# Weight sums of the down product: in place on VectorE instead of on GpSimd

## The chip, the cores and the metric

The kernel runs on one core of one Trainium2 chip. The metric is the device time of one execution in microseconds (us), the median of several runs. The engines are PE (matrix products), PEld (its weight loads), ACT (ScalarE), DVE (VectorE), POOL (GpSimd) and SP, whose queue issues the DMAs.

## What is computed

One block of a hybrid decoder in float32: 16 meta tokens and 1024 tokens of 1024 features, a state-space mixer and differential attention side by side, a merge, and then a gated feed-forward stage with a short convolution. The change lies in the last product of that stage, `@ w_down`:

```python
D_FF = ((8 * D_MODEL // 3 + 127) // 128) * 128      # 2816 = 22 blocks of 128

def conv_glu_ffn(h, w_up, conv_w, conv_b, w_down):
    seq_len = h.shape[1]
    up = h @ w_up
    a, b = up[..., :D_FF], up[..., D_FF:]
    a_pad = jnp.pad(a, ((0, 0), (CONV_W - 1, 0), (0, 0)))
    c = (a_pad[:, 0:seq_len] * conv_w[0] + a_pad[:, 1:seq_len + 1] * conv_w[1]
         + a_pad[:, 2:seq_len + 2] * conv_w[2] + conv_b)
    return (jax.nn.gelu(c) * b) @ w_down

h = h + conv_glu_ffn(rmsnorm(h, norm2_g[l]), w_up[l], conv_w[l], conv_b[l], w_down[l])
```

## The kernel before

Features lie on the partitions, tokens in the columns. Products in float32 accuracy are made of three matmuls: each operand is split in a high part (a copy on ACT, line 103) and a low part (a subtraction on VectorE, line 91), and high times high, high times low and low times high are added up in PSUM.

`ffn_up` (line 961) makes the up product with Strassen's scheme in Winograd's form: `Quad` objects, each with seven products. VectorE adds the products out of PSUM (`plus`, tiles `u2` to `u4` and `T`), GpSimd multiplies the gated halves (`times`, `crow<-crow,T`) and then forms three mixtures of the result (`mix`, tiles `T`), which SP stores to DRAM as `d_act`, `d_t2`, `d_t3`, `d_t4`.

`ffn_down` (line 1022) uses the same scheme for the down product. The weight `w_down` comes as 22 blocks `wd` of 128 x 1024, one DMA each; block f holds the left half of the columns (A11(f), 512 wide) and the right half (A21(f)); block f + 11 holds A12(f) and A22(f). The seven products run in this order, with these weights:

1. A11
2. S3 = A11 - A21
3. A12
4. A22
5. S2 = A21 + A22 - A11
6. S1 = A21 + A22, which the kernel before keeps in A21's place
7. S4 = A12 - S2, in A12's place

Each product is a loop over 11 steps f (`product`, line 1052). A step loads 128 x 512 of data (`act`, SP), splits it into `bop` (ACT, then VectorE), splits the weight into `wop` (`wop`, line 1014: ACT, then VectorE) and issues 12 matmuls of 512 columns into four PSUM tiles (line 181). In the program's order PE has the four high-times-high matmuls of a step first, then those with low parts (from f = 2 of the first product on). `bop` has two buffers (tag R of `rowp`) in the first product and five in the others (R and three of tag bo); `wop` has six. At a product's end ACT or VectorE adds the four PSUM tiles to the running sums (`quarter`, `h`).

Before the change the sums are made by GpSimd, at the place in the code where the product that uses them asks for its weight:

```python
def S3(f):
    s = self.wp.tile([128, 8, 128], F32, tag="raw", name="s3")[:, 0:4]
    self.tt(s, A11(f), A21(f), ALU.subtract, eng=G)
    return s
```

S3 goes into one of two buffers (tag raw), and S2 and S4 are formed in place. A scheduler sets the order of each engine's instructions from these data dependences: in it GpSimd's sums for S2 and S4 stand as soon as their operands are there, between those for S3.

Of the kernel before, what the change touches and what calls it, by code (L numbers as in the profile page):

```python
# [18 lines left out]
T = NM + SEQ  # L19
# [48 lines left out]
class Pool:  # L68
    """A tile pool whose tags have the numbers of buffers given."""
# [13 lines left out]
class Block:  # L83
# [24 lines left out]
    def splitter(self, i):  # L108
        """The engine that takes the low part of the i-th weight block after the attention's start."""
        return self.nc.gpsimd if i >= POOL_FROM else None  # L110

    def load_w(self, ap, eng=None):
        """A weight block of 128 partitions x 1024 columns, split in two parts of 12 bits each."""
# [9 lines left out]
    def mm3(self, ps, terms):  # L123
        """ps = sum of w^T b over (w_hi, w_lo, b_hi, b_lo), in float32 accuracy."""
        n = 3 * len(terms)
        i = 0
        for wh, wl, bh, bl in terms:
            for w, b in ((wh, bh), (wh, bl), (wl, bh)):
                self.nc.tensor.matmul(out=ps, lhsT=w, rhs=b, start=(i == 0), stop=(i == n - 1))  # L129
                i += 1  # L130
# [4 lines left out]
    def split(self, src, hi, lo, scale=None):  # L135
        """hi + lo = src * scale, each of 12 significant bits."""
# [7 lines left out]
    def rms_row(self, acc, n, e_row=None):  # L144
        """The row of 1 / rms on every partition, from the sum of squares over the feature tiles
        (a Newton step on the tables' value of v ** -0.5)."""
# [17 lines left out]
    def lin(self, jobs, tag="mm", late=0):  # L164
        """jobs: (columns, terms) each; one PSUM tile each, all of them open at once; the last `late` terms of
        every job come after the others."""
# [101 lines left out]
    def start(self):  # L268
        """Loads, the splits of h, the first two blocks of u (by k, as h comes in), and the row of 1 / rms."""
# [80 lines left out]
    def qk_block(self, h, qk):  # L350
        """Columns of q or k, normed over the 64 of each half; -2 times them, in fact (the gains make up for it)."""
# [44 lines left out]
    def fill_lin(self, jobs, tiles=None, late=0, outer=False):  # L396
        """As lin, as a generator that yields after the products of each k their time in us; ends with the tiles."""
# [16 lines left out]
    def gates(self):  # L414
        self.wnext = self.load_w(self.a["w_in"][16])
        for i in range(16):
# [16 lines left out]
            else:  # L433
                # by k, so that y takes the places of h as they come free
# [15 lines left out]
    def exp_small(self, x, n, pool, want_em1=None):  # L450
        """exp(x) for x [128, n] (clamped to [-87, 88]); with want_em1 [128, m]: exp(x) - 1 of the first m."""
# [23 lines left out]
    def small_params(self):  # L475
        """lam, and the gains with the constants that go with them."""
# [23 lines left out]
    def ssm(self):  # L500
# [37 lines left out]
        # unit phases and powers 1, 2, 4, 8  # L538
# [31 lines left out]
        # f = (lambda - 1) / a  # L570
# [19 lines left out]
        # signs: the upper half of the partitions holds real parts, the lower imaginary ones  # L590
# [7 lines left out]
        for b in range(4):  # L598
# [11 lines left out]
            # rotation tables e^{i phi (j + 1)}  # L610
# [18 lines left out]
            # Z[states, (m, c')] = lambda^m B  # L629
# [11 lines left out]
            # C lambda^(n+1)  # L641
# [9 lines left out]
            # the kernel's first 8 lags  # L651
# [22 lines left out]
            # chunk inflows, rotated into a frame in which the states only decay  # L674
# [39 lines left out]
    def load_y(self):  # L714
# [7 lines left out]
        # twice gelu, by tanh  # L722
# [58 lines left out]
    def attention(self, fill):  # L781
        """Per step: the scores of one block of queries, the weighted values of the one before, and other
        products between them, as many as hide the softmax."""
# [84 lines left out]
    def w_o(self):  # L868
        """h2 = h + mixed w_o, the first half of the tokens before the second; its rows end up normed."""
# [60 lines left out]
    def operand(self, pool, tag, src, eng=None):  # L930
        """src in two parts of 12 bits each."""
# [6 lines left out]
    def mixtures(self):  # L938
        """The operands of h for the seven products of Strassen's scheme in Winograd's form, the halves being
        those of the features and those of the tokens (which overlap by the two that the convolution needs)."""  # L940
# [73 lines left out]
    def wop(self, w):  # L1014
        """A weight operand of four tiles, in two parts of 12 bits each."""
# [6 lines left out]
    def ffn_down(self):  # L1022
        """The same scheme over halves of the hidden features, of the columns and of the tokens."""
# [14 lines left out]
        def S3(f):  # L1038
            s = self.wp.tile([128, 8, 128], F32, tag="raw", name="s3")[:, 0:4]
            self.tt(s, A11(f), A21(f), ALU.subtract, eng=G)  # L1040
            return s

        def S2(f):
            self.tt(A21(f), A21(f), A22(f), ALU.add, eng=G)
            self.tt(A11(f), A21(f), A11(f), ALU.subtract, eng=G)
            return A11(f)

        def S4(f):
            self.tt(A12(f), A12(f), A11(f), ALU.subtract, eng=G)
            return A12(f)  # L1050

        def product(w, src):
            tiles = [self.psum("mm", [128, n]) for _ in range(4)]
            for f in range(NQ):
# [13 lines left out]
                for m in range(4):  # L1068
                    self.mm3_term(tiles[m], (wh[:, m], wl[:, m], t[:, 0], t[:, 1]), f == 0, f == NQ - 1)
            return tiles  # L1070
# [14 lines left out]
        tiles = product(A11, act(0, 0))  # L1085
# [399 lines left out]
```

## Time and profile before

| | us |
|---|---|
| median of 3 runs | 1481.39 |
| lowest, highest | 1480.11, 1489.38 |
| span of the profiled execution, first to last instruction | 1480.3 |
| first matmul of the down product (line 181, 512 columns) | 1252.44 |
| end of its last matmul | 1474.6 |

The profiled execution's own time is given by its span alone; the median of the runs is 1.1 us above it. Times in the views are counted from the start of the span. A row of a timeline gives the start, the length, the engine, the line (L91 is the helper for VectorE's and GpSimd's two-operand instructions, L103 that for ACT, L129 and L181 are matmuls), what is written and what is read, and in brackets the idle time before it with what ended it. Where a row says x3, its length covers all three. Tile names there have no numbers: `s` is the sum S3, `wd` a weight block or a sum in its place.

### The profile page before, as it was taken

The numbers are of one execution on the slowest core, as the hardware profiler recorded it, in microseconds if no ns is written. First come the engines' busy times: TensorE is split into PE (matmuls) and PEld (weight loads), VectorE is DVE, ScalarE is ACT, GpSimd is POOL, SyncE is SP. The second block draws the span as 40 slices with busy tenths as digits, with TensorE's granted clock in tenths as the row PEclk, the third lists the DMA queues.
The fourth block names the chain that finished last, engine by engine and source line by source line (L and its number), as shares of the span: only waits on it lengthen the run. The fifth ranks groups of instructions, "written<-read, shape, count | busy, mean of one in ns | idle before, by whom it ended". The sixth has DMA issues, their size and how long they took to land.

```text
span 1480.3 us, 23053 instructions
## 1 busy us (share of the span) xinstructions
PE 1419.1 (96%) x8714; PEld 1305.3 (88%) x8714; DVE 1033.7 (70%) x1838; ACT 612.2 (41%) x1144; POOL 601.7 (41%) x517
## 2 busy tenths in 40 slices
PE   8979998999999899999999699999999999989998
PEld 7979898999999798999998698999999998767887
DVE  8948677535646778548366997767767676888574
ACT  6233443345545476433253443333333332433442
POOL 2176565321111301000224666555655557695030
PEclk9999999999999999999999799999999999999999
DMA  5423433472433424567432022233333336925341
GB/s 193 140 75 110 125 112 106 138 187 72 111 104 106 122 67 139 171 237 247 136 129 93 30 78 97 98 107 100 101 107 107 108 114 261 381 70 163 122 128 57
DMA packets 75615, 190.48 MB, mean 129 GB/s; under 512 B 9072, under 2 KB 20720, under 8 KB 75504
## 3 DMA queue, kind: packets, MB, share of 16 engines
q1 hardware_dynamic: 75504, 189.01, 39.7%
q8 instruction: 68, 1.11, 0.3%
q14 instruction: 43, 0.35, 0.1%
HBM read 130.13 MB, written 53.41 MB: 124 GB/s over the span
## 4 chain that ended last, share of the span: by engine, by line
PE 66%; DVE 12%; DMA 7%; POOL 6%; issue 4%; ACT 3%; SPq 2%; DVEq 0%; ACTq 0%; POOLq 0%
PE ps_mm L181 32%; PE ps_mm L129 26%; PE po L1355 3%; POOL rot L91 1%; POOL COS L91 1%; PE s L1319 1%; PE wt L1364 1%; POOL SIN L91 1%; PE s L1320 1%; DMA act<-d_t 1%; DVE wop L91 1%; POOL wd L91 1%; DVE B L91 1%; DMA zs<-z 1%; DMA qkvrow<-d_qkv 1%
## 5 line engine op out<-in xcount | busy, mean ns | idle before, releaser
L129 PE MATMUL ps_mm<-B,wop 128*128 128x256 f32 (+2 forms) x2772 | 443.8, 323 | 14.5 <-DVE B L91 6.8
L129 PEld LDWEIGHTS ps_mm<-B,wop 128*128 128x128 f32 x2772 | 401.4, 192 | 56.6 <-DVE B L91 8.1
L181 PE MATMUL ps_mm<-bop,wop 128*128 128x512 f32 x924 | 215.0, 393 | 9.2 <-DVE bop L91 5.5
L181 PEld LDWEIGHTS ps_mm<-bop,wop 128*128 128x128 f32 x924 | 172.8, 187 | 51.2 <-DVE bop L91 6.3
L181 PE MATMUL ps_mm<-hhi,whi 128*128 128x342 f32 (+2 forms) x432 | 138.3, 331 | 1.8 <-ACT hhi L103 1.8
L181 PE MATMUL ps_mm<-hlo,whi 128*128 128x342 f32 (+2 forms) x432 | 139.6, 323 | 0.1
L181 PE MATMUL ps_mm<-hhi,wlo 128*128 128x342 f32 (+2 forms) x432 | 139.1, 323 | 0.0
L91 POOL TENSOR_TENSOR wlo<-wraw,whi 128x1024 fp32r<-128x1024 f32 x18 | 44.7, 2481 | 205.6 <-ACT whi L103 190.2
L91 POOL TENSOR_TENSOR crow<-crow,T 128x512 f32<-128x512 f32 x44 | 69.8, 1599 | 112.8 <-DVE T L91 112.8
L129 PE MATMUL ps_mm<-hhi,whi 128*128 128x348 f32 (+3 forms) x336 | 113.0, 336 | 0.0
L129 PE MATMUL ps_mm<-hlo,whi 128*128 128x348 f32 (+3 forms) x336 | 110.5, 329 | 0.0
L129 PE MATMUL ps_mm<-hhi,wlo 128*128 128x348 f32 (+3 forms) x336 | 110.1, 328 | 0.0
L91 DVE TENSOR_TENSOR wop<-S,wop 128x512 fp32r<-128x512 f32 x66 | 64.9, 984 | 63.0 <-ACT wop L103 63.0
L91 DVE TENSOR_TENSOR bop<-act,bop 128x512 fp32r<-128x512 f32 x77 | 77.0, 1006 | 39.4 <-ACT bop L103 39.4
L103 ACT ACTIVATE whi<-wraw 128x1024 fp32r<-128x1024 f32 (+3 forms) x62 | 62.1, 1003 | 98.4 <-PE ps_mm L181 49.5
L91 DVE TENSOR_TENSOR wop<-wraw,wop 128x512 fp32r<-128x512 f32 x88 | 86.9, 991 | 13.7 <-ACT wop L103 13.2
L103 ACT ACTIVATE wop<-S 128x512 fp32r<-128x512 f32 x66 | 40.0, 626 | 133.4 <-POOL S L91 96.5
L1321 DVE CUSTOM_DVE_ANT_0 S<-s,bias 128x348 f32<-128x348 f32 (+9 forms) x120 | 57.7, 483 | 51.1 <-PE s L1320 50.6
L91 POOL TENSOR_TENSOR acc<-acc,sq 128x514 f32<-128x514 f32 (+1 forms) x12 | 20.2, 1682 | 171.8 <-ACT sq L103 171.8
L103 ACT ACTIVATE bop<-act 128x512 fp32r<-128x512 f32 x77 | 48.0, 630 | 100.8 <-PE ps_mm L181 100.7
L103 ACT ACTIVATE wop<-wraw 128x512 fp32r<-128x512 f32 x88 | 54.1, 627 | 75.5 <-PE ps_mm L129 53.5
L181 PEld LDWEIGHTS ps_mm<-hhi,whi 128*128 128x128 f32 x432 | 81.5, 191 | 2.9 <-ACT hhi L103 2.3
(311 smaller groups left out, 3294.1 us busy)
## 6 DMA issues: line engine op xcount, KB each, us to landing
wraw<-in_w_up SPq DMA_DIRECT2D x47, 512.0 KB, 3.5
wraw<-in_w_in SPq DMA_DIRECT2D x30, 512.0 KB, 4.2
d_act<-crow SPq DMA_DIRECT2D x22, 512.0 KB, 2.9
act<-d_act SPq DMA_DIRECT2D x44, 256.0 KB, 3.6
wd<-in_w_down SPq DMA_DIRECT2D x22, 512.0 KB, 8.7
d_t<-T SPq DMA_DIRECT2D x33, 256.0 KB, 3.9
act<-d_t SPq DMA_DIRECT2D x33, 256.0 KB, 3.7
d_gate<-gate SPq DMA_DIRECT2D x16, 513.0 KB, 5.1
```

Source lines behind the costliest of these rows:

```text
L91: (eng or self.nc.vector).tensor_tensor(out=out, in0=in0, in1=in1, op=op)
L103: self.nc.scalar.activation(out, in_, func, **kw)
L129: self.nc.tensor.matmul(out=ps, lhsT=w, rhs=b, start=(i == 0), stop=(i == n - 1))
L181: self.nc.tensor.matmul(out=ps, lhsT=w, rhs=b, start=first and i == 0, stop=last and i == 2)
L1319: nc.tensor.matmul(out=ps, lhsT=q, rhs=self.KH[j][:, c0m:c0m + cm], start=True, stop=False)
L1320: nc.tensor.matmul(out=ps, lhsT=q, rhs=self.KL[j][:, c0m:c0m + cm], start=False, stop=True)
L1321: nc.vector.tensor_tensor_reduce(out=s[0:M, c0:c0 + cn], in0=ps[0:M, off:off + cn], in1=self.bias[0:M, b0 + c0:b0 + c0 + cn], scale=1.0, s ...
L1355: nc.tensor.matmul(out=po[0:M], lhsT=l, rhs=rr, start=(kk == 0), stop=(kk == nb))
L1364: nc.tensor.transpose(ps[:, r], w[:, NM + 128 * kk:NM + 128 * (kk + 1)], b.ident)
```

## The change

The functions S2, S3 and S4 go. Four new ones form the same weights in place, on VectorE, and `product` calls one of them after the matmuls of each step: S3 during product 1, S2 during product 3, S1 during product 4, S4 during product 6. S2 is now A22 - S3, S1 is S2 + A11, in A11's place, and products 5 and 6 read them from there. GpSimd forms no weight sum of the down product any more, and the buffers of tag raw are not used there. Docstrings and comments are gone as well; they leave blank lines, so that the lines behind `ffn_down`'s start move by one at most.

```diff
-        def S3(f):
-            s = self.wp.tile([128, 8, 128], F32, tag="raw", name="s3")[:, 0:4]
-            self.tt(s, A11(f), A21(f), ALU.subtract, eng=G)
-            return s
-
-        def S2(f):
-            self.tt(A21(f), A21(f), A22(f), ALU.add, eng=G)
-            self.tt(A11(f), A21(f), A11(f), ALU.subtract, eng=G)
-            return A11(f)
-
-        def S4(f):
-            self.tt(A12(f), A12(f), A11(f), ALU.subtract, eng=G)
-            return A12(f)
+        def to_s3(f):
+            self.tt(A21(f), A11(f), A21(f), ALU.subtract)
+
+        def to_s2(f):
+            self.tt(A21(f), A22(f), A21(f), ALU.subtract)
+
+        def to_s1(f):
+            self.tt(A11(f), A21(f), A11(f), ALU.add)
+
+        def to_s4(f):
+            self.tt(A12(f), A12(f), A21(f), ALU.subtract)
 
-        def product(w, src):
+        def product(w, src, then=None):
...
+                if then is not None:
+                    then(f)
             return tiles
...
-        tiles = product(A11, act(0, 0))
+        tiles = product(A11, act(0, 0), to_s3)
...
-        for m, ps in enumerate(product(S3, lambda f: self.d_t3[f])):
+        for m, ps in enumerate(product(A21, lambda f: self.d_t3[f])):
...
-        for m, ps in enumerate(product(A12, act(1, 0))):
+        for m, ps in enumerate(product(A12, act(1, 0), to_s2)):
...
-        for m, ps in enumerate(product(A22, lambda f: self.d_t4[f])):
+        for m, ps in enumerate(product(A22, lambda f: self.d_t4[f], to_s1)):
...
-        for m, ps in enumerate(product(S2, lambda f: self.d_t2[f])):
+        for m, ps in enumerate(product(A21, lambda f: self.d_t2[f])):
...
-        for m, ps in enumerate(product(A21, act(0, 1))):
+        for m, ps in enumerate(product(A11, act(0, 1), to_s4)):
...
-        for m, ps in enumerate(product(S4, act(1, 1))):
+        for m, ps in enumerate(product(A12, act(1, 1))):
```

The scheduler moves the new instructions on VectorE ahead of where the code has them; PE's order is the same before and after, and on the other engines nothing moves but what stands near the down product.

The first place is VectorE at the start of the down product, from the last addition `T` of the up product to the low part of the data of f = 4. Before (blocks 5 to 7 are `wd_13384`, `wd_13406`, `wd_13427`; `bop_13317`, `bop_13338`, `bop_13360` are the data of f = 2, 3, 4):

```order
L91 TENSOR_TENSOR T_13249<-ps_mm_13236,u3_13158 128x512
L91 TENSOR_TENSOR wop_13386<-wd_13384,wop_13386 128x512
L91 TENSOR_TENSOR bop_13317<-act2_13315,bop_13317 128x512
L91 TENSOR_TENSOR wop_13408<-wd_13406,wop_13408 128x512
L91 TENSOR_TENSOR bop_13338<-act2_13315,bop_13338 128x512
L91 TENSOR_TENSOR wop_13429<-wd_13427,wop_13429 128x512
L91 TENSOR_TENSOR bop_13360<-act2_13358,bop_13360 128x512
```

After (block 5 is `wd_13389`, block 6 `wd_13412`, block 7 `wd_13434`, blocks 8 to 10 `wd_13457`, `wd_13479`, `wd_13502`; the data of f = 2, 3, 4 are `bop_13319`, `bop_13341`, `bop_13364`):

```order
L91 TENSOR_TENSOR T_13249<-ps_mm_13236,u3_13158 128x512
L91 TENSOR_TENSOR wop_13391<-wd_13389,wop_13391 128x512
L91 TENSOR_TENSOR wd_13457<-wd_13457 128x512
L91 TENSOR_TENSOR bop_13319<-act2_13317,bop_13319 128x512
L91 TENSOR_TENSOR wop_13414<-wd_13412,wop_13414 128x512
L91 TENSOR_TENSOR wd_13479<-wd_13479 128x512
L91 TENSOR_TENSOR bop_13341<-act2_13317,bop_13341 128x512
L91 TENSOR_TENSOR wd_13502<-wd_13502 128x512
L91 TENSOR_TENSOR wop_13436<-wd_13434,wop_13436 128x512
L91 TENSOR_TENSOR bop_13364<-act2_13362,bop_13364 128x512
```

The sums S3 of blocks 8, 9 and 10 (`wd_13457<-wd_13457` and so on) now stand between the splits; the eight of blocks 0 to 7 stand in the same way between the rows before these.

The second place is VectorE around the end of the first product. Before, from the low part of the data of the second product's f = 1 (`bop_13547`) to that of its f = 0 (`bop_13525`); `bop_13489` is the data of f = 10 of the first product, and the `s3` are GpSimd's sums:

```order
L91 TENSOR_TENSOR bop_13547<-act_13545,bop_13547 128x512
L91 TENSOR_TENSOR bop_13569<-act2_13567,bop_13569 128x512
L91 TENSOR_TENSOR wop_13574<-s3_13572,wop_13574 128x512
L91 TENSOR_TENSOR bop_13590<-act2_13567,bop_13590 128x512
L91 TENSOR_TENSOR bop_13489<-act_13487,bop_13489 128x512
L91 TENSOR_TENSOR wop_13595<-s3_13593,wop_13595 128x512
L91 TENSOR_TENSOR bop_13525<-act_13523,bop_13525 128x512
```

After, between the same two (`bop_13556`, `bop_13536`); `bop_13499` is f = 10 of the first product, and `wd_13762`, `wd_13785`, `wd_13808` are blocks 11, 12, 13:

```order
L91 TENSOR_TENSOR bop_13556<-act_13554,bop_13556 128x512
L91 TENSOR_TENSOR wd_13277<-wd_13762,wd_13277 128x512
L91 TENSOR_TENSOR bop_13576<-act2_13574,bop_13576 128x512
L91 TENSOR_TENSOR wop_13579<-wd_13322,wop_13579 128x512
L91 TENSOR_TENSOR wd_13277<-wd_13277 128x512
L91 TENSOR_TENSOR bop_13595<-act2_13574,bop_13595 128x512
L91 TENSOR_TENSOR wd_13299<-wd_13785,wd_13299 128x512
L91 TENSOR_TENSOR bop_13499<-act_13497,bop_13499 128x512
L91 TENSOR_TENSOR wop_13598<-wd_13344,wop_13598 128x512
L91 TENSOR_TENSOR wd_13322<-wd_13808,wd_13322 128x512
L91 TENSOR_TENSOR wd_13299<-wd_13299 128x512
L91 TENSOR_TENSOR bop_13536<-act_13534,bop_13536 128x512
```

Ahead of `bop_13499` there are now three sums more: S2 and S1 of f = 0 (`wd_13277`) and S2 of f = 1 (`wd_13299`). S2 of f = 2 (`wd_13322`) and S1 of f = 1 follow behind it. The order goes on like this, with all 11 sums for S2 and all 11 for S1 before the third product's splits begin in earnest, and the 11 for S4 within the third product.

The third place is GpSimd in the second product of the kernel before, where the sums S3 (`s3`) and the two sums for S2 (`wd`) of other blocks take turns; all these rows are gone after:

```order
L91 TENSOR_TENSOR s3_13615<-wd_13363 128x512
L91 TENSOR_TENSOR wd_13320<-wd_13320,wd_13817 128x512
L91 TENSOR_TENSOR s3_13636<-wd_13384 128x512
L91 TENSOR_TENSOR wd_13298<-wd_13298 128x512
L91 TENSOR_TENSOR wd_13341<-wd_13341,wd_13839 128x512
L91 TENSOR_TENSOR wd_13320<-wd_13320 128x512
L91 TENSOR_TENSOR s3_13658<-wd_13406 128x512
```

## Rows read from the trace of the kernel before

**Rows 1.** The page: span, and busy us (share of the span) xinstructions.
```profile
span 1480.3 us, 23053 instructions
...
PE 1419.1 (96%) x8714; PEld 1305.3 (88%) x8714; DVE 1033.7 (70%) x1838; ACT 612.2 (41%) x1144; POOL 601.7 (41%) x517
```

**Rows 2.** PE's timeline: start us, us, instruction xcount, idle before it and releaser.
```profile
1252.44 28.77 PE L181 MATMUL ps_mm<-bop,wop 128*128 128x512 f32 x124
1283.47 27.17 PE L181 MATMUL ps_mm<-bop,wop 128*128 128x512 f32 x116 [2.26 <-DVE bop L91]
1312.18 5.82 PE L181 MATMUL ps_mm<-bop,wop 128*128 128x512 f32 x24 [1.54 <-ACT wop L103]
1320.18 11.59 PE L181 MATMUL ps_mm<-bop,wop 128*128 128x512 f32 x49 [2.19 <-ACT wop L103]
1334.98 10.24 PE L181 MATMUL ps_mm<-bop,wop 128*128 128x512 f32 x43 [3.20 <-DVE bop L91]
```

**Rows 3.** The chain that ended last, its end: start us, us, what.
```profile
1334.98 139.61 PE ps_mm L181 x602
1474.60 0.02 issue
1474.62 2.73 DVE quarter L91 x4
```

**Rows 4.** ACT's timeline, the copies that waited for GpSimd's sum.
```profile
1311.49 0.63 ACT L103 ACTIVATE wop<-s 128x512 fp32r<-128x512 f32 x1 [4.65 <-POOL s L91]
...
1319.50 0.63 ACT L103 ACTIVATE wop<-s 128x512 fp32r<-128x512 f32 x1 [5.29 <-POOL s L91]
```

**Rows 5.** Windows: PE, PEld, DVE, ACT, POOL busy, PEclk, DMA share, GB/s.
```profile
1320.00:1351.00 31.00, 27.61 (x118) 22.14 (x119) 30.85 (x24) 13.64 (x25) 29.49 (x18) 1.00 0.22 68
...
1382.00:1413.00 31.00, 31.00 (x135) 25.05 (x135) 16.52 (x26) 12.87 (x23) 0.00 (x0) 1.00 0.40 130
```

**Rows 6.** VectorE by shape, 1300 to 1351: xcount, busy us, mean ns.
```profile
L91 DVE TENSOR_TENSOR wop<-wd,wop 128x512 fp32r<-128x512 f32 x12 | 21.3, 1778 | 0.0
...
L91 DVE TENSOR_TENSOR quarter<-ps_mm,quarter 128x512 f32<-128x512 f32 x4 | 2.5, 675 | 0.0
```

**Rows 7.** VectorE's timeline, GpSimd at rest.
```profile
1261.99 0.68 DVE L91 TENSOR_TENSOR bop<-act,bop 128x512 fp32r<-128x512 f32 x1
1262.59 0.68 DVE L91 TENSOR_TENSOR wop<-wd,wop 128x512 fp32r<-128x512 f32 x1
```

**Rows 8.** GpSimd by shape, 1270 to 1351: xcount, busy us, mean ns.
```profile
L91 POOL TENSOR_TENSOR wd<-wd 128x512 f32<-128x512 f32 x33 | 54.0, 1660 | 1.5 <-DVE wop L91 1.4
L91 POOL TENSOR_TENSOR s<-wd 128x512 f32<-128x512 f32 x9 | 14.6, 1621 | 13.1 <-DVE wop L91 13.1
```

**Rows 9.** VectorE's timeline before the first stall of PE.
```profile
1275.44 5.10 DVE L91 TENSOR_TENSOR bop<-act,bop 128x512 fp32r<-128x512 f32 x3 [1.48 <-ACT bop L103]
1280.46 0.68 DVE L91 TENSOR_TENSOR wop<-s,wop 128x512 fp32r<-128x512 f32 x1
1281.07 2.35 DVE L91 TENSOR_TENSOR bop<-act,bop 128x512 fp32r<-128x512 f32 x2
```

**Rows 10.** ACT's timeline, copies of data operands that waited for PE.
```profile
1258.17 0.63 ACT L103 ACTIVATE bop<-act 128x512 fp32r<-128x512 f32 x1 [1.61 <-PE ps_mm L181]
...
1280.31 0.63 ACT L103 ACTIVATE bop<-act 128x512 fp32r<-128x512 f32 x1 [1.62 <-PE ps_mm L181]
```

**Rows 11.** SP's timeline, and under each its last issue's KB, us to landing.
```profile
1248.93 1.61 SPq L1031 DMA_DIRECT2D wd<-in_w_down  x2
wd<-in_w_down SPq DMA_DIRECT2D x1, 512.0 KB, 7.7
...
1268.28 1.60 SPq L1031 DMA_DIRECT2D wd<-in_w_down  x3
wd<-in_w_down SPq DMA_DIRECT2D x1, 512.0 KB, 7.2
```

**Rows 12.** GpSimd's timeline, the last mix.
```profile
1253.41 1.74 POOL L91 TENSOR_TENSOR crow<-crow,T 128x512 f32<-128x512 f32 x1 [0.22 <-DVE T L91]
...
1259.88 1.64 POOL L91 TENSOR_TENSOR T<-crow,T 128x512 f32<-128x512 f32 x1
```

## The prediction

> **What bounds the kernel now.** First the page's busy times: PE has 96% of the 1480.3 us span, VectorE 70%, GpSimd 41% [rows 1]. So a change on VectorE or GpSimd is worth only the time in which PE stands still, and the question is where it does so near the edit. The second view is PE's timeline from the end of the up product on [rows 2]. The down product starts at 1252.44 us (the first matmul of line 181), and from there PE is idle four times: 2.26, 1.54, 2.19 and 3.20 us, 9.19 us together, the last one ending at 1334.98. From that moment the chain that ended last is one unbroken piece of PE until 1474.60, and then 2.73 us of VectorE additions [rows 3]. Hence the whole of what this change can give back is 9.2 us, all of it between 1281 and 1335, in the first three of the seven products.
>
> The releasers in [rows 2] name two kinds. Two waits (1.54 and 2.19) are for ACT's copy of a weight operand. ACT's timeline shows what that copy waited for: `wop<-s`, 4.65 and 5.29 us, released by GpSimd's sum `s` [rows 4]. The other two (2.26 and 3.20) are for VectorE's low part of a data operand, `bop`. VectorE is 30.85 us busy in the 31 us from 1320, but only 16.52 us in the 31 us from 1382, where one product does the same splits [rows 5]. The difference is the duration of single instructions: `wop<-wd` with two inputs in SBUF takes 1.778 us on average from 1300 to 1351, while the additions from PSUM in the same stretch take 0.675 [rows 6]. With GpSimd at rest the same splits take 0.68 and start 0.60 us apart [rows 7]. From 1270 to 1351 GpSimd runs 33 sums into `wd` and 9 into `s`, 68.6 us in an 81 us stretch [rows 8]. So both kinds of stall come from GpSimd's sums: they are late themselves, and they stretch VectorE's splits.
>
> **Removed.** 44 GpSimd sums of 128x512 (33 `wd`, 11 `s`; [rows 8] show 42 of them at 1.62 to 1.66 us). With them goes GpSimd's lateness (the two stalls behind `s`, 3.73 us) and, from 1270 on, the stretching of VectorE's splits (the two behind `bop`, 5.46 us). After the last mix GpSimd has only the additions of h. The gain is at most 3.73 + 5.46 = 9.19 us.
>
> **Added.** 44 VectorE sums of the same size, both inputs in SBUF, as the splits have. The trace has no such sum on VectorE, so I bound it by the split: 0.60 us of VectorE's time per instruction with GpSimd at rest [rows 7], 1.70 us (three in 5.10) beside GpSimd [rows 9]. I take 0.61 after GpSimd's last mix and the upper end before it.
>
> In the second product the order of the changed kernel gives VectorE 22 splits and 22 sums (11 to S2, 11 to S1). PE's step of one f is (1280.31 - 1258.17) / 8 = 2.77 us, by the copies that wait for PE [rows 10], so a product takes 11 x 2.77 = 30.5 us. VectorE needs 44 x 0.61 = 26.8 us: it fits, with 3.7 to spare. In the third it has 22 splits, 11 sums (S4) and 4 additions from PSUM, 37 x 0.61 = 22.6. GpSimd's four additions of h now fall into the second product; at 1.7 us each they hold VectorE for 6.8 us, in which it gets 4 instructions done and not 11, a loss of 4.3 us. The prepared operands cover it: bop has five buffers from there on, four steps ahead, 11 us. I cost it at nothing.
>
> The step that stalled for 2.26 us is f = 10 of the first product. PE runs four matmuls of a step from the high part before it needs the low one, so f = 10, which starts at 1280.31 [rows 10], needs it at 1281.2; that is where PE stopped. VectorE then had three bop at 1.70 each and finished it at 1283.4 [rows 9]. In the changed order three sums stand ahead of it as well: nine instructions from 1275.44, at 0.61 each, end at 1280.9. That is 0.3 us before the need. I cost it at nothing.
>
> **Where the sums queue in front of something.** VectorE takes its work in order, so a sum that waits for its weight block holds what stands behind it. Behind S3 of blocks 9 and 10 stand bop of f = 3 and 4, behind S2 of the first three blocks f = 10. Block 10 is issued as the second transfer of the pair at 1248.93 and lands 7.7 us later, by about 1258 [rows 11]. Block 13 is the third issued from 1268.28 and lands 7.2 us after its issue, at 1276.7 [rows 11], while its S2 would run at about 1281.6. So 4.9 us of cover there, and none to speak of for blocks 9 and 10.
>
> In the first product bop turns over only two buffers (tag R), so each low part can start only one step ahead: 2.77 + 0.92 us from ACT's start to PE's need. For f = 3 that is 1258.17 [rows 10] to about 1261.9. GpSimd's last mix runs from 1253.41 to 1261.5 [rows 12] and stays where it is, or comes a little later, for VectorE's additions into T now stand behind S3 sums. From the last T at about 1254.0, VectorE has wop, S3 of block 8, bop of f = 2, wop, S3 of block 9, bop of f = 3. If each takes 1.70 until GpSimd ends and 0.6 then, f = 2 is done at 1259.1 (need 1258.9) and f = 3 at 1263.1 (need 1261.9): 0.2 + 1.2 = 1.4 us of new stall. If none is stretched, nothing. With T another 0.6 later, 2 us or a little more. I take 1.2, since VectorE is seen stretched in most of that stretch.
>
> **Sum.** 9.2 - 1.2 = 8.0 us. The profiled span becomes 1480.3 - 8.0 = 1472.3. The median of the runs shown is 1481.39, 1.1 above that span; with the same distance the prediction is 1473.4 us, 0.54% less. Its own range: 1472.2 (no new stall) to 1475.
>
> **Rival 1, VectorE becomes the bound (slower side).** Place: the second and third product. For it: VectorE is full from 1320 on [rows 5], and the change gives it more. Its price hangs on the mean distance s between its instructions there: 44 s + 37 s against 2 x 30.5 us of PE. At 0.61 there is room. The loss is 81 s - 61 us, and it eats the 8.0 us at s = 0.85. At s = 1.0 it is 20 us, 1473.4 + 20 = 1493; from 1.04 on the kernel is over 1% slower. Against it: [rows 7] against [rows 6], the same instruction at 0.68 and 1.78 with GpSimd's presence as the difference, and PSUM inputs not stretched. 10%.
> The Trainium skill, Perfetto Trace Analysis, section Optimizing Scalar/DVE Operations, says that with a saturated VectorE offloading to ScalarE or even GpSimd may make sense, though the two share a read port of SBUF, so that moving work between them might not help. By its first half the change goes the wrong way, and this rival is what would follow; by its second half VectorE's full slices are no saturation of its own, and the trace agrees with that (1.78 us against 0.68).
>
> **Rival 2, a stall stays.** The 2.26 us at f = 10 hang on a margin of 0.3 us, and everything in the first product that comes later shifts it. If that stall stays, 1473.4 + 2.3 = 1475.7. For it: two buffers of bop. Against it: the sum of nine instructions above. 12%.
>
> **Rival 3, late weight blocks.** The additions into T wait behind S3, so the mix, its stores and all loads behind them in SP's queue come X later. Up to X = 4.9 the cover of the S2 sums takes it; beyond, each us is a us of PE. At X = 10 the time is 1473.4 + 5.1 = 1478.5, and at X = 13 the gain is gone. For it: the transfers land only 7 to 8 us after their issue there [rows 11]. Against it: my X from the rows is about 1. 8%.
>
> **That the change does not do what it says:** the order shows the sums in place and a product ahead, and GpSimd without them; only where VectorE has no time would they come late, which is rival 1.
>
> **How the numbers follow.** Forecast 66%, rival 1 10%, rival 2 12%, rival 3 8%; 4% for what I do not see, such as a PE pace that changes. About 1%, 14.8 us, is what a measurement of this kernel can tell from no change. No case of mine gains that: the whole idle time is 9.2 us, so over 1% faster gets 4%. Over 1% slower is rival 1 with s above 1.04, half of it, 5%. The rest, 91%, is within 1%. The range for 8 in 10 begins at 1471.0, 1.2 below the case without any new stall, for the scatter of the runs, and reaches to 1480.0, which takes in rivals 2 and 3 and leaves out most of rival 1.
>
> **What would show it.** Right: PE from 1252 on with less than 2.5 us of idle time, all of it before 1270; `wop<-wd` on VectorE at 0.68 us from 1265 to 1285; no GpSimd work between its last mix and the additions of h; the same unbroken chain of PE to the end, 8 us earlier. Wrong: PE waiting for `bop` in the second or third product while VectorE is full (rival 1), for `bop` at the end of the first (rival 2), or VectorE idle in front of a `wd` sum with a transfer as releaser (rival 3).

## The result and the profile after

The changed kernel takes 1476.79 us in the median of five runs (1472.78 to 1477.98). The kernel before, run beside it, takes 1484.38 (five runs, 1480.11 to 1489.38). The ratio is 0.994, with a 95% interval from 0.9922 to 0.9958: 7.6 us or 0.5% faster, and so within 1%, as was forecast.

The page of the changed kernel, which answers to [rows 1]:

```profile
span 1476.2 us, 23032 instructions
...
PE 1420.2 (96%) x8714; PEld 1305.5 (88%) x8714; DVE 1032.7 (70%) x1882; ACT 611.7 (41%) x1144; POOL 543.5 (37%) x473
```

GpSimd has 44 instructions less and VectorE 44 more, yet VectorE's busy time is 1.0 us less than before. 44 added sums cost it nothing in total, because its other instructions in this stretch became shorter.

PE's timeline over the down product (start us, us, instruction xcount, idle before it and releaser), which answers to [rows 2]:

```profile
1254.20 9.78 PE L181 MATMUL ps_mm<-bop,wop 128*128 128x512 f32 x40
1266.04 206.46 PE L181 MATMUL ps_mm<-bop,wop 128*128 128x512 f32 x884 [2.06 <-DVE bop L91]
```

All four stalls of before are gone, and a new one of 2.06 us stands behind matmul 40. A step has 12 matmuls, so that is f = 3 of the first product, four matmuls in. From 1266.04 on PE never waits again. The end of the chain that ended last, which answers to [rows 3]:

```profile
1266.04 204.44 PE ps_mm L181 x875
1470.48 0.02 issue
1470.50 2.73 DVE quarter L91 x4
```

VectorE and GpSimd by shape (xcount, busy us, mean ns), VectorE from 1265 to 1285 and then GpSimd from 1266 to 1351, which answer to [rows 6] and [rows 8]:

```profile
L91 DVE TENSOR_TENSOR bop<-act,bop 128x512 fp32r<-128x512 f32 x9 | 7.2, 806 | 7.9 <-ACT bop L103 7.9
L91 DVE TENSOR_TENSOR wop<-wd,wop 128x512 fp32r<-128x512 f32 x7 | 4.8, 682 | 0.0
L91 DVE TENSOR_TENSOR wd<-wd 128x512 f32<-128x512 f32 x3 | 2.0, 681 | 0.0
```

```profile
L91 POOL TENSOR_TENSOR h<-h,quarter 128x512 f32<-128x512 f32 x4 | 15.5, 3907 | 28.6 <-DMA h<-d_h 28.6
```

The weight splits have come down from 1778 to 682 ns, and the new sums `wd<-wd` take 681, as the splits do. In 85 us GpSimd does four instructions. The 31 us from 1320, which answer to [rows 5] (PE, PEld, DVE, ACT, POOL busy, PEclk, DMA share, GB/s):

```profile
1320.00:1351.00 31.00, 31.00 (x135) 25.06 (x135) 22.86 (x37) 13.12 (x24) 0.00 (x0) 1.00 0.32 104
```

VectorE does 37 instructions there and is 22.86 us busy; before, it did 24 and was 30.85 us busy.

To compare executions I use the length of the down product, from its first matmul to the end of its last in PE's timeline. It is 1266.04 + 206.46 - 1254.20 = 218.30 us here. Before, the last piece of PE's timeline starts at 1334.98 and is 141.64 us long, so it ends at 1476.62 and the length is 224.18 us; the 1474.60 of [rows 3], which the table of times gives as the end of the last matmul, is where the chain passes from PE to VectorE. PE goes from the up product into the down product without a gap in both profiles, so the start of the down product is set upstream; it lies between 1248.95 and 1257.35 in the executions below, so the total of a single run says less than this length.

### The profile page after: what moved, and what is told of

It is laid out like the page before. It is cut to its first block, busy times and chain, and to the rows that moved or that the text cites. A ratio compares the mean times of both kernels' runs of the same rounds, so it can differ in the third digit from the quotient of the medians.

```text
span 1476.2 us, 23032 instructions
## 1 busy us (share of the span) xinstructions
PE 1420.2 (96%) x8714; PEld 1305.5 (88%) x8714; DVE 1032.7 (70%) x1882; ACT 611.7 (41%) x1144; POOL 543.5 (37%) x473
## 4 chain that ended last, share of the span: by engine, by line
PE 67%; DVE 13%; DMA 7%; POOL 5%; issue 4%; ACT 3%; SPq 2%; DVEq 0%; ACTq 0%; POOLq 0%
PE ps_mm L181 34%; PE ps_mm L129 26%; PE po L1356 2%; POOL rot L91 1%; DVE wop L91 1%; DMA zs<-z 1%; POOL SIN L91 1%; POOL COS L91 1%; PE s L1320 1%; DVE B L91 1%; PE wt L1365 1%; DMA qkvrow<-d_qkv 1%; PE s L1321 1%; DMA wraw<-in_w_up 1%; DMA d_m<-g1row 1%
## 5 line engine op out<-in xcount | busy, mean ns | idle before, releaser
L91 DVE TENSOR_TENSOR wop<-wraw,wop 128x512 fp32r<-128x512 f32 x88 | 91.2, 1040 | 6.6 <-ACT wop L103 6.0
L91 DVE TENSOR_TENSOR bop<-act,bop 128x512 fp32r<-128x512 f32 x77 | 59.1, 769 | 47.8 <-ACT bop L103 47.8
L181 PEld LDWEIGHTS ps_mm<-hlo,whi 128*128 128x128 f32 x432 | 82.6, 191 | 0.8 <-DVE hlo L100 0.5
```

The source lines that it names most:

```text
L91: (eng or self.nc.vector).tensor_tensor(out=out, in0=in0, in1=in1, op=op)
L181: self.nc.tensor.matmul(out=ps, lhsT=w, rhs=b, start=first and i == 0, stop=last and i == 2)
```

## The experiments

Theory A is the prediction's: GpSimd's sums cost PE time because two engines work on two SBUF inputs at once, so that VectorE's splits take 1.78 us in place of 0.68. Theory B is the rival: what helped is the placement, a product ahead of the use, so that nothing is late.

**1. Placement without the engine, and the engine without the placement.** The first run keeps the changed order, with the four sums put back on GpSimd:

```diff
-            self.tt(A21(f), A11(f), A21(f), ALU.subtract)
+            self.tt(A21(f), A11(f), A21(f), ALU.subtract, eng=G)
...
-            self.tt(A12(f), A12(f), A21(f), ALU.subtract)
+            self.tt(A12(f), A12(f), A21(f), ALU.subtract, eng=G)
```

> The changed kernel with its 44 sums put back on GpSimd, still in place and a product ahead. Theory A (GpSimd's sums harm twice: they come late, and they stretch VectorE's splits from 0.68 to 1.78 us): the lateness goes, the stretching stays. In the second and third product VectorE has 22 splits at about 1.7 us, 37 us against 30.5 us of PE, so PE is idle 5 to 10 us in the down product, all of it behind bop or wop of VectorE, none behind a GpSimd sum; the time lies within 3 us of the kernel before. Theory B (the place a product ahead gives the gain, the engine does not matter): PE idle under 3 us and the time of the changed kernel.

The second is the kernel before, with `eng=G` taken out of S2, S3 and S4 and nothing else:

```diff
-            self.tt(s, A11(f), A21(f), ALU.subtract, eng=G)
+            self.tt(s, A11(f), A21(f), ALU.subtract)
...
-            self.tt(A12(f), A12(f), A11(f), ALU.subtract, eng=G)
+            self.tt(A12(f), A12(f), A11(f), ALU.subtract)
```

> The kernel before with its sums on VectorE, but at their old places: S3 into the two raw buffers, S2 and S4 where the product that uses them asks for them. Theory A: no stretched splits after GpSimd's last mix and no sum that waits for GpSimd; S3 beyond the first two blocks cannot stand ahead of the first product's data, so the new stall of 2.06 us at f = 3 is gone too: PE idle under 1 us, time 1 to 4 us below the changed kernel. Theory B: the sums come late as before, the two stalls behind s (3.7 us together) stay, time 3 us or more above the changed kernel.

Placement alone gives 1484.16 us against 1484.33, ratio 0.9995 (0.9981 to 1.0009): nothing. PE's timeline of that run, VectorE's splits from 1285 to 1345 by shape, and a window behind the last stall (PE, PEld, DVE, ACT, POOL busy, PEclk, DMA share, GB/s):

```profile
1254.05 12.30 PE L181 MATMUL ps_mm<-bop,wop 128*128 128x512 f32 x52
...
1273.54 10.40 PE L181 MATMUL ps_mm<-bop,wop 128*128 128x512 f32 x44 [0.39 <-DVE bop L91]
1285.51 1.21 PE L181 MATMUL ps_mm<-bop,wop 128*128 128x512 f32 x4 [1.57 <-ACT bop L103]
1290.87 188.15 PE L181 MATMUL ps_mm<-bop,wop 128*128 128x512 f32 x800 [4.16 <-DVE bop L91]
```

```profile
L91 DVE TENSOR_TENSOR wop<-wd,wop 128x512 fp32r<-128x512 f32 x19 | 33.7, 1775 | 0.0
```

```profile
1290.80:1297.60 6.80, 6.73 (x17) 5.34 (x18) 5.77 (x6) 3.42 (x6) 6.17 (x4) 0.55 1.03 403
```

The waits for GpSimd's sums are gone, and still PE stands five times, 6.83 us in all, 5.3 of it behind VectorE's low parts. That is 2.4 us less idle time than before, but behind the longest stall the granted clock is 0.55 over 6.8 us, which takes 3.1 us back. The length is 224.97 us. The stretching is not alone in this. In GpSimd's queue the S3 sums now stand between the instructions of the last mix, which ends at 1272.93, 18.9 us behind the first matmul of the down product (9.1 before), and the data that it stores come back later. ACT waited 3.67 us for them; the row of its waits (us in total, times, longest us):

```profile
ACT bop L103 <- DMA act<-d_t: 3.7, 1, 3.7
```

VectorE stood 3.60 us for ACT in turn, and began at 1283.41 the five instructions that end the stall of 4.16 us. They took 7.4 us; at 0.60 us apart they would have been done by about 1286.5 (an estimate), ahead of the moment, 1286.72, at which PE stopped. So the stall of 1.57 us, behind ACT, comes from the late data, and the longest from these and the stretching together.

VectorE with the old placement gives 1474.81 us, ratio 0.9934 (0.9911 to 0.9956), and PE does not wait once:

```profile
1256.43 214.22 PE L181 MATMUL ps_mm<-bop,wop 128*128 128x512 f32 x924
```

Theory B falls: the engine is the whole of the gain, and the placement of the change even costs something, the new stall, for with the old placement the length is 214.22 us. Theory A stands so far; that the stretching by itself costs PE time, with nobody waiting for GpSimd, is shown by experiment 5.

**2. The new stall.** The prediction put it on S3 of the late blocks, which stand ahead of the low parts of f = 2 and 3. This run holds S3 of blocks 8 to 10 behind the splits of their own steps:

```diff
-            self.tt(A21(f), A11(f), A21(f), ALU.subtract)
+            ins = nc.vector.tensor_tensor(out=A21(f), in0=A11(f), in1=A21(f), op=ALU.subtract)
+            if f >= 8:
+                self.tc.keep_in_program_order(ins)
```

> The changed kernel with S3 of blocks 8, 9 and 10 held on VectorE behind the splits of their own step. Theory A' (the new stall of 2.06 us is the price of two sums, 1.78 and 1.80 us, ahead of the data of f = 3 while GpSimd's last mix still runs, and the half clock of PE from 1268.0 to 1271.4 follows from that stall): stall gone, no half clock there, the first product 30.5 us long instead of about 34.8, time 2 to 4 us below the changed kernel. Rival (the data of f = 3 are late by the mix alone): stall of 1 us or more stays.

> The changed kernel once more, beside the other three on one chip. It shows how the stall at f = 3 and PE's clock behind it repeat: with theory A' the stall is there again, 1.5 to 2.5 us, and PE's granted clock falls to one half behind it in some executions; if the stall differs by more than 1 us, it hangs on something that varies from run to run.

It took 1472.55 us, ratio 0.9918 (0.9897 to 0.9939), beside 1477.04 for the changed kernel, 0.9957 (0.9934 to 0.9981). PE's timeline of the first, then of the changed kernel run beside it:

```profile
1252.66 213.98 PE L181 MATMUL ps_mm<-bop,wop 128*128 128x512 f32 x924
```

```profile
1255.03 6.63 PE L181 MATMUL ps_mm<-bop,wop 128*128 128x512 f32 x28
1261.83 3.03 PE L181 MATMUL ps_mm<-bop,wop 128*128 128x512 f32 x12 [0.17 <-DVE bop L91]
1266.92 204.85 PE L181 MATMUL ps_mm<-bop,wop 128*128 128x512 f32 x884 [2.05 <-DVE bop L91]
```

So the stall is those sums' doing: without them ahead it is gone, with PE in one piece. Since the intervals of the two overlap a little, both were run again:

> The changed kernel with S3 of blocks 8 to 10 held behind the splits of their own steps, a second time with more rounds. If the new stall at f = 3 is what is left to gain, PE runs the down product in one piece of 214 us, and the time is 2 to 4.5 us below the changed kernel run beside it, 1470 to 1475. If the first measurement was the scatter of the start of the down product (1252 to 1256 us), the two medians agree within 1.5 us.

> The changed kernel itself, beside the version with S3 held: 1475 to 1478, with a stall of about 2 us at f = 3 and none later.

1473.28 us, ratio 0.9925 (0.9898 to 0.9952), against 1477.76, ratio 0.9943 (0.9922 to 0.9965). PE's timeline of the first, then of the changed kernel:

```profile
1253.95 213.93 PE L181 MATMUL ps_mm<-bop,wop 128*128 128x512 f32 x924
```

```profile
1254.27 6.63 PE L181 MATMUL ps_mm<-bop,wop 128*128 128x512 f32 x28
1262.39 3.06 PE L181 MATMUL ps_mm<-bop,wop 128*128 128x512 f32 x12 [1.49 <-DVE bop L91]
1267.47 204.81 PE L181 MATMUL ps_mm<-bop,wop 128*128 128x512 f32 x884 [2.02 <-DVE bop L91]
```

The two medians are 4.5 us apart both times, and the lengths are 213.93 against 218.01. In this third profile of the changed kernel PE also stands 1.49 us behind matmul 28, which is the low part of f = 2; the second had 0.17 us there and the first nothing. The ratios against the kernel before overlap both times. But in the first comparison every run of this version (1471.13 to 1474.05) lies below every run of the changed kernel (1475.25 to 1482.77), the distance came twice, and the stall is there in every trace of the one (2.06, 2.05, 2.02 us) and in neither of the other. So this version is faster than the changed kernel. From the sums on VectorE at their old places (1474.81 us, a length of 214.22) it cannot be told apart here.

**3. How much sharing VectorE bears.** S3 alone on VectorE, with S2, S1 and S4 on GpSimd at the changed places:

```diff
-            self.tt(A21(f), A22(f), A21(f), ALU.subtract)
+            self.tt(A21(f), A22(f), A21(f), ALU.subtract, eng=G)
-            self.tt(A11(f), A21(f), A11(f), ALU.add)
+            self.tt(A11(f), A21(f), A11(f), ALU.add, eng=G)
-            self.tt(A12(f), A12(f), A21(f), ALU.subtract)
+            self.tt(A12(f), A12(f), A21(f), ALU.subtract, eng=G)
```

> The changed kernel with S3 on VectorE and S2, S1 and S4 on GpSimd, all in place and a product ahead as the change has them. Theory A (what costs is two engines on two SBUF inputs at once: any GpSimd sum beside the splits stretches them): GpSimd has 33 sums left, some 33 x 1.65 = 54 us of them in the second and third product; wop<-wd on VectorE is again near 1.75 us there, and PE stands still for bop in the second product, where S2 and S1 fall, 3 us or more beside the 2.06 us at f = 3 of the first; the time lies between the changed kernel and the kernel before, 1479 to 1485. Theory B (only the late sums mattered, and only those in front of the first product's end, which are S3's): no PE idle time behind 1270, and the time of the changed kernel, 1475 to 1478.

One run, 1474.69 us, below both windows; the kernel before took 1482.47 beside it, also in one run. Its down product began at 1248.95, 5.3 us ahead of the changed kernel's profile, and its length of 220.28 us lies between the two kernels. PE's timeline, then its splits from 1283 to 1317:

```profile
1248.95 9.81 PE L181 MATMUL ps_mm<-bop,wop 128*128 128x512 f32 x40
1260.78 21.24 PE L181 MATMUL ps_mm<-bop,wop 128*128 128x512 f32 x84 [2.02 <-DVE bop L91]
1283.15 3.06 PE L181 MATMUL ps_mm<-bop,wop 128*128 128x512 f32 x12 [1.13 <-DVE bop L91]
1286.54 182.69 PE L181 MATMUL ps_mm<-bop,wop 128*128 128x512 f32 x788 [0.33 <-DVE bop L91]
```

```profile
L91 DVE TENSOR_TENSOR wop<-wd,wop 128x512 fp32r<-128x512 f32 x11 | 19.6, 1778 | 0.0
```

The stretching is there as theory A says, but it costs PE only 1.46 us behind the first stall, not 3: VectorE has 33 sums less to do there, and none of the sums left on GpSimd is waited for. As a test of theory B on the total it is inconclusive; the two stalls behind 1270 speak against B.

**4. VectorE's room.** Two runs add sums to VectorE in the steps of the second product, with results that nothing reads (the 4 is a 2 in the first):

```diff
+        def extra(f):
+            for _ in range(4):
+                j = self.wp.tile([128, 8, 128], F32, tag="raw", name="junk")[:, 0:4]
+                self.tc.keep_in_program_order(
+                    nc.vector.tensor_tensor(out=j, in0=A12(f), in1=A22(f), op=ALU.add))
...
-        for m, ps in enumerate(product(A21, lambda f: self.d_t3[f])):
+        for m, ps in enumerate(product(A21, lambda f: self.d_t3[f], extra)):
```

> The changed kernel with 2 more VectorE sums of the same size per step of the second product, 22 in all, into buffers that nothing reads; what the kernel computes is unchanged. It measures how much room VectorE has left there, which the rival of the prediction (VectorE becomes the bound, a loss of 81 s - 61 us over the second and third product) puts in numbers: with 22 more the formula is 103 s - 61. At s = 0.60, the spacing seen with GpSimd at rest, it is 61.8 - 61, a loss of about 1 us at most, which the splits prepared ahead cover: PE idle under 1 us behind 1270 and the time of the changed kernel within 2 us (theory A: there was room). At s = 0.75 it is 16 us of loss (theory C: the changed kernel stood near the edge).

> The changed kernel with 4 more VectorE sums per step of the second product, 44 in all, into buffers that nothing reads; what the kernel computes is unchanged. By the formula of theory A the second and third product need 125 x 0.60 = 75 us of VectorE against 61 us of PE; within the second product alone 88 x 0.60 = 52.8 against 30.5, 22 us too much, of which operands prepared ahead cover up to about 11. So PE stands still for 11 to 22 us, behind bop, in the second product, and the time is 1488 to 1499. Theory C (s = 0.75): 66 - 30.5 - 11 = 24 us or more, 1501 or later. If the time stays within 3 us of the changed kernel, the formula is wrong and VectorE has far more room than it says.

They took 1479.28 and 1477.29 us, with lengths of 218.11 and 220.22. The run with 44 more, by PE's timeline, then by windows:

```profile
1262.72 22.18 PE L181 MATMUL ps_mm<-bop,wop 128*128 128x512 f32 x88 [1.77 <-DVE bop L91]
1286.13 2.12 PE L181 MATMUL ps_mm<-bop,wop 128*128 128x512 f32 x8 [1.23 <-DVE bop L91]
1289.14 182.64 PE L181 MATMUL ps_mm<-bop,wop 128*128 128x512 f32 x788 [0.89 <-DVE bop L91]
```

```profile
1286.00:1320.00 34.00, 32.98 (x141) 26.47 (x142) 34.00 (x58) 15.58 (x28) 29.45 (x1) 1.00 0.52 187
1320.00:1351.00 31.00, 31.00 (x135) 25.09 (x134) 31.00 (x49) 12.92 (x23) 7.26 (x4) 1.00 0.36 114
```

VectorE is busy without a gap for 65 us here, and PE in full work beside it from 1289.14 on. The 11 to 22 us of stall did not come. My expectation was wrong in one term: it took the extra sums as due within the second product, but the last of them runs at 1377.4, so that 44 x 0.60 = 26 us were spread over more than three products. What it does show: 26 us of VectorE's time were free there, which the changed kernel left unused. The two small stalls (1.23 and 0.89) are at f = 10 of the first product, eight matmuls in, and just behind it; the run with 22 more has 1.22 and 0.28 us there. In both runs four of the extra sums stand ahead of that low part, 2.4 us at 0.60 each; the prediction had found a margin of only 0.3 us, and PE gets four matmuls (0.9 us) further here before it needs the part, which leaves 1.2.

**5. GpSimd beside VectorE with nobody waiting for it.** Three GpSimd sums per step of the second product, into the same unread buffers, so that only GpSimd's presence is added:

```diff
+        def extra(f):
+            for _ in range(3):
+                j = self.wp.tile([128, 8, 128], F32, tag="raw", name="junk")[:, 0:4]
+                self.tt(j, A12(f), A22(f), ALU.add, eng=G)
```

> The changed kernel with 3 sums of 128x512 on GpSimd per step of the second product, 33 in all, into buffers that nothing reads: GpSimd can be late there for nobody, so only its presence beside VectorE is added. What the kernel computes is unchanged. Theory A (GpSimd's sums stretch VectorE's splits and sums by turns, one for one): while GpSimd works, VectorE's instructions come 1.7 us apart; the second product's 44 then take up to 75 us against 30.5, so PE stands still for 10 us or more behind bop, and the time is 1487 or later. Theory D (a VectorE that works back to back shuts GpSimd out, as the 10.40 us addition of h in the changed kernel suggests): GpSimd's sums take several us each, VectorE's stay near 0.6 to 0.7 while its queue is full, PE idles under 4 us behind 1270, and the time is 1476 to 1481.

1506.88 us, 30 above the changed kernel and 24 above the one run of the kernel before beside it: theory A's figures, not theory D's. PE's piece behind the first long stall, VectorE's sums from 1287.7 to 1337 by shape, and that window:

```profile
1296.70 3.78 PE L181 MATMUL ps_mm<-bop,wop 128*128 128x512 f32 x8 [9.03 <-DVE bop L91]
```

```profile
L91 DVE TENSOR_TENSOR wd<-wd 128x512 f32<-128x512 f32 x15 | 26.0, 1768 | 0.0
```

```profile
1287.70:1337.00 49.30, 30.80 (x101) 22.73 (x101) 49.30 (x30) 12.08 (x22) 49.30 (x31) 0.79 0.30 111
```

30 VectorE and 31 GpSimd instructions share 49.3 us, one for one. VectorE gets one done per 1.64 us and PE gets 101 matmuls where its unstalled pace (214 us for 924) would give 213. This is the prediction's first rival at work, with GpSimd as the cause that stretches s. Its PE idle time behind 1270 is 20.48 us, and the clock adds to that: 0.79 was granted in this window against 1.00 without stalls.

GpSimd had started here while VectorE was idle. The last run lets it start inside a run of VectorE, with the three sums behind each S2 in place of `extra`:

```diff
             self.tt(A21(f), A22(f), A21(f), ALU.subtract)
+            for _ in range(3):
+                j = self.wp.tile([128, 8, 128], F32, tag="raw", name="junk")[:, 0:4]
+                self.tt(j, A21(f), A22(f), ALU.add, eng=G)
```

> The changed kernel with 3 sums of 128x512 on GpSimd behind each S2, 33 in all, into buffers that nothing reads; what the kernel computes is unchanged. As many GpSimd sums as in the run before with 3 per step of the second product, but each waits for a sum of VectorE, so GpSimd becomes ready only inside VectorE's run of back-to-back instructions. Theory A2 (the two take turns whenever both have work): alternation 1.7 us apart from about 1282 on, PE stands still behind bop for 10 us or more behind 1270, and the time is 1490 or later, as there (1506.88). Theory D2 (who is inside a back-to-back run keeps the other out, and turns begin only at a gap of VectorE): GpSimd's first sum takes 15 us or more, VectorE stays 0.60 us apart until a gap or a group of PSUM additions at 1300 or later, the turns begin there, when operands are prepared far ahead; PE idle behind 1270 is under 8 us and the time 1476 to 1488.

1512.33 us: theory D2 falls. VectorE's timeline around GpSimd's first sum, which started at 1284.94:

```profile
1284.72 0.69 DVE L91 TENSOR_TENSOR bop<-act,bop 128x512 fp32r<-128x512 f32 x1
1285.32 1.79 DVE L91 TENSOR_TENSOR wop<-wd,wop 128x512 fp32r<-128x512 f32 x1
```

The turns begin after a single instruction of VectorE.

## Why the prediction was right, and where its terms were off

**What goes.** Right. All four stalls of [rows 2] are gone, those behind GpSimd's sum and those behind stretched splits. The worth was a little more than the 9.2 us summed: 224.18 - 213.95 = 10.2 us of length against the unstalled piece (the mean of the two runs of experiment 2). The clock was 1.00 through those stalls, so 1.0 us is lost beside the idle time itself, some 0.26 us per stall; that is an estimate from this difference. The second and third profiles of the changed kernel, at 1.00 too, give 0.28 and 0.27 per stall in the same way (216.74 and 218.01 us, two stalls each).

**Which cause.** Right, and now shown for the engine: with placement alone nothing is gained, with the engine alone all of it. That the stretching by itself costs PE time is shown by the 20.48 us of experiment 5. How the 9.19 us divide between lateness and stretching stays open: with the late sums [rows 4] out of the way the waits behind `bop` came to 5.3 us, near the 5.46 of before, but the longest of them hung on late data as well, so that the closeness is partly chance.

**44 sums hidden on VectorE.** Right: 0.60 us apart with GpSimd at rest, and 26 us of room were left. GpSimd's additions of h cost nothing, as forecast, though not by the working given: the first was held off for 10.40 us and stretched nothing meanwhile.

**f = 10, margin 0.3 us.** Right: no stall there in the changed kernel, and one of about 1.2 us as soon as four sums more stand ahead.

**The new stall at f = 3.** Right in its place and its cause, too small in its size: 1.2 us taken, 2.06 measured, and 2.22 and 3.51 us of idle time there in the two other profiles, the last of them beyond the 2.5 us that the prediction named as its sign of being right. The term that failed is the end of GpSimd's last mix, taken as unmoved or "a little later". VectorE's timeline, then the last instruction of the mix in GpSimd's, in the changed kernel:

```profile
1255.71 0.68 DVE L91 TENSOR_TENSOR T<-ps_mm,u 128x512 f32<-128x512 f32 x1
...
1262.52 1.80 DVE L91 TENSOR_TENSOR wd<-wd 128x512 f32<-128x512 f32 x1
1264.24 1.75 DVE L91 TENSOR_TENSOR bop<-act,bop 128x512 fp32r<-128x512 f32 x1
```

```profile
1263.85 1.59 POOL L91 TENSOR_TENSOR T<-crow,T 128x512 f32<-128x512 f32 x1
```

The mix ends at 1265.44, 11.2 us behind the first matmul of the down product; before it was 9.1 [rows 2, 12]. It holds VectorE's instructions at 1.70 us apart up to and including the low part of f = 3, which is done at 1265.99, 11.8 us behind the first matmul; the prediction's sum had 10.7 (1263.1), with that last instruction at 0.6. The last addition into T starts 1.5 us behind the first matmul, where it was 0.2 before, and the mix ends 9.7 us behind that addition, where it was 8.9. The prediction moved T and left the end of the mix in its place. S3 of blocks 8 and 9 do not lengthen the mix by much: in both runs that hold them back (experiment 2) it still ends 10.7 us behind the first matmul. What they cost is their own two turns of 1.70 us ahead of the low part of f = 3.

The upper end of that term, "2 us or a little more", with T another 0.6 us later, is what happened: the instruction behind the last T starts at 1256.31, 2.11 us behind the first matmul, where the sum had 1.56. In the third profile it is 3.50 us, and there the low part of f = 2 comes late too.

**A term that was missing: PE's clock behind the new stall.** By windows of the changed kernel:

```profile
1266.00:1268.00 2.00, 1.96 (x7) 1.65 (x8) 2.00 (x4) 0.00 (x0) 0.00 (x0) 0.84 0.40 114
1268.00:1271.40 3.40, 3.40 (x10) 2.60 (x10) 1.69 (x3) 1.15 (x2) 0.00 (x0) 0.59 0.96 320
1271.40:1284.80 13.40, 13.40 (x60) 10.89 (x58) 7.17 (x12) 7.34 (x13) 0.00 (x0) 1.00 1.03 388
```

The granted clock is 0.59 over 3.4 us, so most of that stretch is at 1.2 GHz and not 2.4. That costs 0.16 x 2.0 + 0.41 x 3.4 = 1.7 us. In the two other profiles of the same kernel the stall was as long and 1.00 was granted behind it. Experiments 3 to 5 have five more profiles with this stall (1.77 to 2.02 us): in three of them 0.50 was granted over 2 us behind it, in two 1.00.

**The sum.** 8.0 us were forecast. By lengths, against the one profile of the kernel before, the change brings 5.9 us in its own profile and 7.4 and 6.2 in the two others; by medians it brings 7.6, 7.3 and 7.4. The forecast median, 1473.4, is 3.4 below the measured one. 3.0 of that is where it started: 1481.39 was the median of three runs, 1484.38 is that of five. The measured median lies above the forecast's own range (to 1475) and inside the wide one (1471.0 to 1480.0). The prediction took about 1% for what can be told from no change; the interval measured is 0.2% to either side.

**The rivals.** The first (VectorE as the bound) did not come about, but its price was real: with GpSimd kept busy it cost 30 us. The Trainium skill, Perfetto Trace Analysis, section Optimizing Scalar/DVE Operations, leaves open whether moving work from a full VectorE to GpSimd helps; here the trace decides against it, since GpSimd's share is what filled VectorE. The second's stall at f = 10 went. For the third (late weight blocks) nothing speaks: the waits of VectorE from 1252 on are these, none of them for a transfer:

```profile
DVE bop L91 <- ACT bop L103: 47.8, 37, 2.5
DVE quarter L91 <- PE ps_mm L181: 15.2, 4, 10.5
DVE h L91 <- PE ps_mm L181: 1.5, 1, 1.5
```

## What to carry to other kernels

Where an engine looks full, compare the duration of one of its instructions with the same shape at another time: a VectorE 100% busy at 1.78 us per split was held up by its helper, and giving it the helper's work made it less busy (30.85 of 31 us before, 22.86 after). When work is moved ahead of its use, look at what it overtakes at the start of the stage, where few operands are prepared; holding three sums back there gave 4.5 us by medians, 2.8 to 4.4 by the lengths of the down product, on top of the change's 7.6. For changes of this size compare the length of the stage in the trace, since the stage's start alone lay up to 8.4 us apart in the executions here.

## What was not expected of the hardware

Taking turns is not all there is between VectorE and GpSimd. GpSimd's timeline in the changed kernel, then VectorE's from the last of the instructions that passed that addition of h:

```profile
1294.03 10.40 POOL L91 TENSOR_TENSOR h<-h,quarter 128x512 f32<-128x512 f32 x1 [28.59 <-DMA h<-d_h]
```

```profile
1302.59 0.68 DVE L91 TENSOR_TENSOR wop<-wd,wop 128x512 fp32r<-128x512 f32 x1
1303.83 1.15 DVE L91 TENSOR_TENSOR bop<-act,bop 128x512 fp32r<-128x512 f32 x1 [0.56 <-ACT bop L103]
1304.91 1.78 DVE L91 TENSOR_TENSOR wd<-wd 128x512 f32<-128x512 f32 x1
```

An instruction that takes 1.74 us in turns took 10.40, while 15 of VectorE's passed it 0.60 us apart, and it came to its end only with VectorE's first gap, of 0.56 us. In the run with 44 more VectorE sums, where VectorE had no gap, the same addition took 31.60 us and ended at 1322.15, just behind VectorE's first addition out of PSUM (1320.92 to 1321.60). Yet in the last run of experiment 5 GpSimd got its turn after one instruction of VectorE. The Trainium skill, SBUF — State Buffer, section Who interferes with whom, says that a VectorE instruction with two SBUF inputs contends with a GpSimd instruction that reads SBUF, that the shared ports are an exclusive lock, and that the order of issue decides who blocks. The turns of 1.64 us agree with that; the 10.40 and 31.60 us do not, if the lock is held for one instruction at a time, for then GpSimd would have had its turn after one. What decides between the two ways stays open; the operands differ as well (rows of 512 in the additions of h, blocks of 4 x 128 in the added sums), and no run separates that.

The half clock behind the stall of about 2 us at f = 3 came in four of the eight profiles that have this stall, among them one of the three of the changed kernel; what decides that was not tried either.
